# A decoder trunk on one Trainium2 core: a first pass with the scale's dot first, weights split behind the last heads, and modulation dots at other places

## The chip, the cores and the metric

The kernel runs on one core of a Trainium2 chip. The metric is device time in microseconds (us) for one execution, taken as the median of several runs; lower is better. A core has five engines that run their own instruction streams in order: TensorE (PE; its weight loads are listed as PEld), VectorE (DVE), ScalarE (ACT), GpSimd (POOL), and SyncE (SP), which here only issues DMAs. They meet at semaphores. An instruction that waits holds everything behind it on its engine.

## The reference

Two decoder layers on 256 tokens of width 1024, float32. Layer 0 mixes tokens by three dilated sliding-window attentions (16 heads of 64), layer 1 by gated linear attention (GLA, 4 heads, chunks of 64). A gated ConvFFN (inner width 2816) follows each. Every sub-layer is normed and modulated by a conditioning vector c:

```python
mod = silu(c) @ w_ada[i] + b_ada[i]
sh1, sc1, g1, sh2, sc2, g2 = split(mod, 6)
h = rmsnorm(x, norm_mix[i]) * (1 + sc1) + sh1
x = x + g1 * mixer(h)                  # attention, or GLA
h = rmsnorm(x, norm_ffn[i]) * (1 + sc2) + sh2
x = x + g2 * conv_ffn(h)
```

The modulation weights w_ada are 2 x 1024 x 6144 floats: 48 MB that are read once and used for a single vector.

## The kernel before, in words

Tokens lie along the free axis, features on the partitions, in KT = 8 tiles of 128 x 256. Every big product is done in three float32r products (`mm3`, lines 178 to 183): ScalarE rounds an operand to its high part (a cast, line 172), VectorE subtracts to get the low part (line 175), and TensorE adds high x high, low x high and high x low. So each weight chunk costs a DMA into one of four `raw` buffers, two casts on ScalarE (`whi`) and two subtractions on VectorE (`wlo`), all in `split` (line 156); `whi` and `wlo` have six buffers each.

Modulation isn't done on TensorE. `ada_chunk` (line 129) loads 1 MB of w_ada and does two dots with silu(c) on VectorE (line 138; a second small instruction reads the sum), and ScalarE adds the bias and makes the 128 x 1 column that the norm uses (lines 146 and 148): of scale or of shift. There are 48 chunks. The first eight make scale and shift of the first norm, one pair for each of the eight input tiles; the other forty are put between other work by `next_ada`.

First pass (lines 360 to 402, and 535 to 545): from the squares of x comes rstd (line 190). Then, for each of the eight input tiles (a block here), a chunk of modulation, `normed` (line 259: xr, high part hhi, low part hlo of the normed tile), and 15 x 128 columns of weights `w0`. A block feeds 42 products of TensorE, for the q, k of two head pairs and the v of one.

Then come eight head pairs (`attend`), the output projection with residual and squares (`project`, line 579), and the FFN (`ffn`, line 613), whose first two weight chunks are split early; the second waits in order behind the sixth tile's scaling (line 615). The norm's mean square is a product of TensorE over summed squares (`sqacc`, then `ms`, line 193).

In layer 1, four chunks of v weights are split and loaded (line 775; `next_ada` behind the third and fourth), then the decay gates, then for each head `states` (line 799): k_d, q_t, k_t from q, k and the gates (lines 818 to 820), k_d turned by TensorE (kdt, line 826), and the running states. `products` and `normed_output` (lines 859 and 873) make a head's output and its norm (osq, oacc, ms, on); `gate` (line 897) makes two tiles of the silu gate from 48 products (pr). Heads' outputs times gates give ohi and olo (lines 942 to 945) for `project`, whose products are py.

The order on each engine is fixed when the program is built: the Tile framework places instructions by its own estimate of time, and `behind(...)` only says that an instruction stands later in its engine's order than another one. It adds no wait.

Of the kernel before, what the change touches and what calls it, by code (L numbers as in the profile page):

```python
# [49 lines left out]

ADA_ORDER = [x for kt in range(KT) for x in ((0, kt), (1, kt))]
ADA_ORDER += [(2, kt) for kt in range(KT)]
# [5 lines left out]
def trunk(ctx: ExitStack, tc: tile.TileContext, I, out):  # L58
# [69 lines left out]

    def ada_chunk(l, n, dmas=1):
        raw = wraw.tile([P, 2048], F32, tag="raw", name="ada_raw")  # L130
        for i in range(dmas):
            c = slice(2048 * i // dmas, 2048 * (i + 1) // dmas)
            nc.sync.dma_start(raw[:, c], I["w_ada"][l, n][:, c])
        for s in range(2):
            piece, kt = ADA_ORDER[2 * n + s]
            dot = tmp.tile([P, 1], F32, tag="dot", name="dot", bufs=4)
            w = raw[:, D * s : D * s + D]
            nc.vector.tensor_tensor_reduce(  # L138
                w, w, c_bc, op0=ALU.mult, op1=ALU.add, scale=1.0, scalar=0.0, accum_out=dot,
            )  # L140
            m = state.tile([P, 1], F32, tag=f"mod{l}{piece}{kt}", name="mod")
            b = col(C_BADA + 48 * l + 8 * piece + kt)
            if piece in (1, 4):
                g = col((C_NMIX if piece == 1 else C_NFFN) + 8 * l + kt)
                b1 = (16 if piece == 4 else 0) + 8 * l + kt
                last = nc.scalar.activation(m, dot, AF.Identity, scale=g, bias=one_b[:, b1 : b1 + 1])
            else:
                last = nc.scalar.activation(m, dot, AF.Identity, bias=b)
            mod[l, piece, kt] = m
        return last  # L150

# [3 lines left out]

    def split(src, n, dmas=1, after=((), ()), late=(), low=(), cut=None):
        cut = cut or (n // 2 if n > 1024 else n)
        raw = wraw.tile([P, 2048], F32, tag="raw", name="raw")
        for c in (slice(0, cut), slice(cut, n)) if dmas > 1 else (slice(0, n),):
            last_load[0] = nc.sync.dma_start(raw[:, c], src[:, c])  # L160
        pieces = []
        for c in (slice(0, cut), slice(cut, n)):
            if c.stop > c.start:
                hi = wspl.tile([P, 1024], F32R, tag="whi", name="whi")
                lo = wspl.tile([P, 1024], F32R, tag="wlo", name="wlo")
                pieces.append((c.start, c.stop, hi, lo, raw[:, c]))
        ops = [(hi[:, 0 : b - a], lo[:, 0 : b - a], r) for a, b, hi, lo, r in pieces]
        if n == 1024:
            ops = [tuple(z[:, c] for z in ops[0]) for c in (slice(0, 512), slice(512, n))]
        for i, (hi, lo, r) in enumerate(ops):  # L170
            with behind(*after[i]):
                copied[0] = nc.scalar.copy(hi, r)  # L172
        for i, (hi, lo, r) in enumerate(ops):
            with behind(*(late if i else low)):
                last_lo[0] = nc.vector.tensor_tensor(lo, r, hi.bitcast(F32), op=ALU.subtract)  # L175
        return pieces

    def mm3(ps, a, b, start, stop):
# [79 lines left out]

    def normed(l, sub, r, kt):

        xr = tmp.tile([P, T], F32, tag="xr", name="xr")
        a, sh = mod[l, 3 * sub + 1, kt], mod[l, 3 * sub, kt]
        nc.vector.scalar_tensor_tensor(xr, x[kt], a[:, 0:1], r, op0=ALU.mult, op1=ALU.mult)
        hi, lo = h_hi[kt][:, :], h_lo[kt][:, :]
        i = nc.scalar.activation(hi, xr, AF.Identity, bias=sh[:, 0:1])  # L265
        j = nc.vector.scalar_tensor_tensor(
            lo, xr, sh[:, 0:1], hi.bitcast(F32), op0=ALU.add, op1=ALU.subtract
        )
        chain[kt] = chain[7] = i, j
        return h_hi[kt], h_lo[kt]  # L270
# [96 lines left out]
    for n in (0, 4):  # L367
        for m in (2, 1):
            s = sq[n // 4]
            last_add = nc.vector.tensor_tensor(s[:, 0:m, :], s[:, 0:m, :], s[:, m : 2 * m, :], op=ALU.add)  # L370
        if n == 0:
            with behind(last_add):
                last_add = scale_terms(0)
    exp_ln_after(last_sq)
    r = rstd_of([s[:, 0, :] for s in sq])

    rows_ps, at = [], 0
    with behind(norm_ops[0]):
        keep_warm(3)
        for i, (g, n) in enumerate(ROWS):  # L380
            c = slice(at, at + n)
            ps = bank("rows", "t")[:16, 0:n]
            rows_ps.append((ps, c))
            mm(ps, tab[:, 16 * g : 16 * g + 16], oh[:33, c], start=True, stop=True)
            at += n
    first = norm_ops[1], last_add
    w0, h = [], []
    for kt in range(KT):
        with behind(*first):
            term = ada_chunk(0, kt, dmas=1 if kt else 2)  # L390
        h.append(normed(0, 0, r, kt))
        if kt:
            w0.append(split(I["w0"][kt], 15 * P, cut=8 * P))
        else:
            with behind(chain[0][1]):
                w0.append(split(I["w0"][kt], 15 * P, 2, cut=8 * P, after=((term,), (chain[0][0],))))
# [3 lines left out]
            first = (last_lo[0],)  # L400
        if kt == 1:
            scale_terms(1)
    with tc.issue_after(last_load[0].ins):
# [11 lines left out]

    last_t, last_po = [None], [None]

    def attend(u, q, k, v, bias):
# [61 lines left out]
        src, hv, lv = in_order(po[:, :T]), as_tokens(hi), as_tokens(lo)  # L480
        nc.scalar.copy(hv, src)
        nc.vector.tensor_tensor(lv, src, hv.bitcast(F32), op=ALU.subtract)
        o_hi.append(hi)
# [35 lines left out]
    for u in range(NPAIR):  # L519
# [10 lines left out]
        if u == 0:  # L530
# [5 lines left out]
            for kt in range(KT):  # L536
                s, e = kt == 0, kt == KT - 1
                for i in range(2 * NG):
                    mm3(pqk[i][:, :T], parts(w0[kt], P * i), h[kt], s and i % 2 == 0, e and i % 2 == 1)
# [4 lines left out]
                for i in range(2 * NG):  # L544
                    mm3(pqk1[i], parts(w0[kt], P * (i + (6 if i < 2 else 9))), h[kt], s and i % 2 == 0, e and i % 2 == 1)
        if u < 2:
# [252 lines left out]
    def states(hd):  # L799
# [24 lines left out]
        for t in range(2):  # L824
            c = slice(P * t, P * t + P)
            nc.tensor.transpose(ps[:, c], k_d[:, c], ident)
        turned_keys[:] = nc.scalar.copy(kd, ps[:, :T]), last_key

        pa = bank("a", "s")
# [42 lines left out]

    def normed_output(hd, po, after=()):
# [3 lines left out]
        nc.vector.tensor_tensor(acc, sq[:, 0:T], sq[:, T : 2 * T], op=ALU.add)  # L877
        with behind(*after):
            rr = rstd_of([acc], 256, "s")
        on = gt([P, 2, T], f"on{hd}")  # L880
# [4 lines left out]

    r_g = []

# [9 lines left out]
    def gate(n):  # L897
        level = level_tiles() if n == 2 else ()

        w = split(I["w_r_b"][n], 2048, **({} if n else dict(after=(turned_keys[:1], ()), low=turned_keys[1:])))  # L900
        pr = bank("pr", "p")
        for kt in range(KT):
            for s in range(2):
                with behind(*((), last_o, norm_ops[:1], ())[n]):
                    mm3(pr[:, T * s : T * s + T], parts(w, 2 * P * kt + P * s),
                        level[kt] if n == 2 and kt < 2 else h[kt], kt == 0 and s == 0, kt == KT - 1 and s == 1)
        r = gt([P, (2, 3)[n % 2] * T], f"r{n}", tag=("r0", "C1", "r2", "cs1")[n])
        r_g.append(r[:, : 2 * T].rearrange("p (a b) -> p a b", a=2))
# [14 lines left out]
    gate(0)  # L923
    for _ in range(3):
        next_ada()
    po3 = products(3, *s3)
    normed_output(2, po2, last_o)
    normed_output(3, po3)
    gate(1)
    next_ada()  # L930
    for n in range(4):

        if n > 1:
            gate(n)
        r = r_g[n]
        if n < 2:
# [161 lines left out]
```

## Time and profile before

| | us |
|---|---|
| median of 3 runs | 791.72 (791.23 to 794.37) |
| the profiled execution | 792.91 |
| its span, first to last instruction | 791.1 |
| outside the span | 1.8 |
| TensorE busy | 772.1 |
| VectorE busy | 647.5 |
| ScalarE busy | 486.9 |

Times in rows are us from the span's start. A row of the timeline reads: start, duration, engine, line, operation, output and inputs by their names in the code, shapes, count (xN: so many in a row, the duration being from the first's start to the last's end), and in brackets the idle time of the engine just before it and what ended it. Pipelined instructions overlap their successors a little, so a step costs the distance of two starts rather than the printed duration. A row of a table of stretches reads: the stretch, its length, for each engine busy us and count, the granted TensorE clock as a share of full speed, the DMA engines' busy share, and GB/s.

### The profile page before, as it was taken

Reading aid. Unit: us, or ns where it says so; the run is one execution under the profiler, and the core shown is the slowest. Engines: PE = TensorE matmul, PEld = TensorE weight load, DVE = VectorE, ACT = ScalarE, POOL = GpSimd, SP = SyncE. Lnnn points to the kernel's source line nnn. Section 1 sums busy time; section 2 is a strip of 40 time slices with the busy share of each in tenths; the row PEclk is TensorE's granted clock in tenths of the full one; section 3 lists DMA queues with packets and bytes.
Section 4 is the critical chain, followed back from the end, with each engine's and each line's share of the span. In section 5 each row is a group of like instructions: output and inputs, shape, how many; then the busy total and the mean of one; then the engine's idle time right before and its main releaser. Section 6 shows DMA issues by size and latency. Waiting matters only on the chain.

```text
span 791.1 us, 15977 instructions
## 1 busy us (share of the span) xinstructions
PE 772.1 (98%) x6416; PEld 744.7 (94%) x6416; DVE 647.5 (82%) x1159; ACT 486.9 (62%) x939; POOL 12.2 (2%) x40
## 2 busy tenths in 40 slices
PE   8799999999999998999999999989999999999997
PEld 5799999999999997999999999888999999999997
DVE  6988988778788958999998776895777998899672
ACT  5546555555545647877666565654776876666551
POOL 1000000000000000000000000000000000000000
PEclk9899999999999999999999999999999999999999
DMA  9998576685775835767645895982544765555741
GB/s 350 418 331 331 157 312 218 232 317 196 270 273 197 302 141 172 285 239 264 218 146 197 301 323 188 329 303 86 214 165 156 258 206 184 206 195 183 274 150 54
DMA packets 32616, 184.72 MB, mean 233 GB/s; under 512 B 5852, under 2 KB 7388, under 8 KB 16286
## 3 DMA queue, kind: packets, MB, share of 16 engines
q1 hardware_dynamic: 32160, 183.26, 65.0%
q8 instruction: 50, 0.82, 0.4%
q10 hardware_dynamic: 382, 0.45, 0.2%
q14 instruction: 24, 0.20, 0.1%
HBM read 182.59 MB, written 1.10 MB: 232 GB/s over the span
## 4 chain that ended last, share of the span: by engine, by line
PE 90%; DVE 4%; ACT 3%; DMA 2%; issue 1%; ACTq 0%; DVEq 0%
PE pab L181 10%; PE pab L183 10%; PE pab L182 10%; PE pqk L181 7%; PE pqk L182 6%; PE pqk L183 6%; PE pd L183 5%; PE pd L182 5%; PE pd L181 5%; PE pv L181 3%; PE pv L183 2%; PE pv L182 2%; PE s L429 2%; PE py L181 2%; PE py L182 2%; PE py L183 2%
## 5 line engine op out<-in xcount | busy, mean ns | idle before, releaser
L172 ACT CAST whi<-raw 128x1024 fp32r<-128x1024 f32 (+3 forms) x273 | 252.5, 949 | 158.3 <-PE pab L182 56.0
L175 DVE TENSOR_TENSOR wlo<-raw,whi 128x1024 fp32r<-128x1024 f32 (+3 forms) x273 | 295.4, 1099 | 62.1 <-ACT whi L172 60.3
L183 PE MATMUL pab<-hhi,wlo 128*128 128x256 f32 x672 | 185.0, 276 | 0.0
L182 PE MATMUL pab<-hlo,whi 128*128 128x256 f32 x672 | 184.9, 276 | 0.0
L181 PE MATMUL pab<-hhi,whi 128*128 128x256 f32 x672 | 183.7, 277 | 0.0
L181 PE MATMUL pqk<-hhi,whi 128*128 128x256 f32 x440 | 122.6, 287 | 5.8 <-ACT hhi L265 5.8
L183 PEld LDWEIGHTS pab<-hhi,wlo 128*128 128x128 f32 x672 | 126.2, 188 | 0.0
L182 PEld LDWEIGHTS pab<-hlo,whi 128*128 128x128 f32 x672 | 126.1, 188 | 0.1
L181 PEld LDWEIGHTS pab<-hhi,whi 128*128 128x128 f32 x672 | 125.3, 188 | 0.1
L182 PE MATMUL pqk<-hlo,whi 128*128 128x256 f32 x440 | 123.6, 284 | 0.0
L183 PE MATMUL pqk<-hhi,wlo 128*128 128x256 f32 x440 | 123.0, 283 | 0.0
L138 DVE CUSTOM_DVE_ANT_0 ada_raw<-ada_raw,c_bc 128x1024 f32<-128x1024 f32 x96 | 113.5, 1219 | 9.6 <-DMA ada_raw<-in_w_ada 9.6
L183 PE MATMUL pd<-ghi,wlo 128*128 128x256 f32 x352 | 97.2, 276 | 0.0
L181 PE MATMUL pd<-ghi,whi 128*128 128x256 f32 x352 | 97.2, 276 | 0.0
L182 PE MATMUL pd<-glo,whi 128*128 128x256 f32 x352 | 97.2, 276 | 0.0
L181 PEld LDWEIGHTS pqk<-hhi,whi 128*128 128x128 f32 x440 | 83.1, 192 | 7.1 <-ACT hhi L265 6.2
L182 PEld LDWEIGHTS pqk<-hlo,whi 128*128 128x128 f32 x440 | 83.7, 191 | 0.8 <-issue 0.3
L183 PEld LDWEIGHTS pqk<-hhi,wlo 128*128 128x128 f32 x440 | 83.6, 191 | 0.5 <-issue 0.3
L181 PEld LDWEIGHTS pd<-ghi,whi 128*128 128x128 f32 x352 | 66.1, 188 | 0.0
L183 PEld LDWEIGHTS pd<-ghi,wlo 128*128 128x128 f32 x352 | 66.1, 188 | 0.0
L182 PEld LDWEIGHTS pd<-glo,whi 128*128 128x128 f32 x352 | 66.1, 188 | 0.0
L182 PE MATMUL pv<-wlo,hhi 128*128 128x384 f32 (+1 forms) x144 | 50.3, 349 | 0.0
(215 smaller groups left out, 1308.2 us busy)
## 6 DMA issues: line engine op xcount, KB each, us to landing
ada_raw<-in_w_ada SPq DMA_DIRECT2D x47, 1024.0 KB, 6.7
raw<-in_w_up SPq DMA_DIRECT2D x42, 1024.0 KB, 4.8
raw<-in_w_down SPq DMA_DIRECT2D x32, 704.0 KB, 5.0
raw<-in_wqk SPq DMA_DIRECT2D x18, 1024.0 KB, 6.7
raw<-in_wv SPq DMA_DIRECT2D x14, 768.0 KB, 4.8
raw<-in_w SPq DMA_DIRECT2D x7, 960.0 KB, 6.9
raw<-in_w_out_a SPq DMA_DIRECT2D x4, 1024.0 KB, 7.3
raw<-in_w_v_b SPq DMA_DIRECT2D x4, 1024.0 KB, 6.9
```

The lines of the kernel that those rows point to most:

```text
L138: nc.vector.tensor_tensor_reduce(w, w, c_bc, op0=ALU.mult, op1=ALU.add, scale=1.0, scalar=0.0, accum_out=dot,)
L172: copied[0] = nc.scalar.copy(hi, r)
L175: last_lo[0] = nc.vector.tensor_tensor(lo, r, hi.bitcast(F32), op=ALU.subtract)
L181: mm(ps, a[0], b[0], start=start, stop=False)
L182: mm(ps, a[0], b[1], start=False, stop=False)
L183: return mm(ps, a[1], b[0], start=False, stop=stop)
L429: mm(s[:, 0:n], q[0][a][:, r].rearrange("p a b -> p (a b)"), k[0][b][:, 0:n], start=(i == 0), stop=(i == 2))
```

## The change

It has these parts:

1. The order of modulation pieces is scale, shift instead of shift, scale. `ada_chunk` is divided into a load and single dots.
2. In the first pass a block's work is ordered by hand: scale's dot, the previous block's second low part, shift's dot, xr, first low part, hlo. In block 0 TensorE does the products with high parts of the normed tile first.
3. The second half of the squares goes to TensorE in four pieces instead of two additions on VectorE; six warm-up products are added ahead of the first pass.
4. The split of the FFN's second weight chunk in layer 0 is put behind the last head pair's output instead of behind the sixth tile's scaling, and its second low part no longer behind the residuals.
5. In layer 1 the six modulation chunks of the v weights and gates are placed behind k_t of heads 0, 1 and 2, behind head 3's sum of squares, and behind the low parts of gates 2 and 3. The norms of heads 2 and 3 come behind both gate(0) and gate(1).

```diff
-ADA_ORDER = [x for kt in range(KT) for x in ((0, kt), (1, kt))]
+ADA_ORDER = [x for kt in range(KT) for x in ((1, kt), (0, kt))]
...
-    r = rstd_of([s[:, 0, :] for s in sq])
+    r = rstd_of([sq[0][:, 0, :]] + [sq[1][:, i, :] for i in range(4)])
...
+    with behind(last_row):
+        keep_warm(6)
     w0, h = [], []
+    ada = ada_load(0, 0, 2)
+    with behind(norm_ops[1], last_add):
+        dots = [ada_dot(0, 0, s, ada) for s in range(2)]
     for kt in range(KT):
-        with behind(*first):
-            term = ada_chunk(0, kt, dmas=1 if kt else 2)
-        h.append(normed(0, 0, r, kt))
-        if kt:
-            w0.append(split(I["w0"][kt], 15 * P, cut=8 * P))
...
+        term = dots[1][1]
+        def between(scaled, high):
+            w0.append(split(I["w0"][kt], 15 * P, 1 if kt else 2, cut=8 * P, after=((term,), (high,)), lows=False))
+            with behind(scaled):
+                return [low_part(w0[-1], 0)]
+        h.append(normed(0, 0, r, kt, (dots[1][0],), between))
+        last = chain[kt][1]
...
+        if kt < KT - 1:
+            ada = ada_load(0, kt + 1)
+            with behind(last):
+                dots = [ada_dot(0, kt + 1, 0, ada)]
+            last = dots[0][0]
+        with behind(last):
+            last = low_part(w0[kt], 1)
...
+        if kt < KT - 1:
+            with behind(last):
+                dots.append(ada_dot(0, kt + 1, 1, ada))
...
-        with behind(*sixth):
-            w_early.append(split(I["w_up"][l, 1], 2048, late=last_x[1:]))
+        with behind(*(sixth if l else o_parts)):
+            w_early.append(split(I["w_up"][l, 1], 2048, late=last_x[1:] if l else ()))
...
             w = split(I["w_v_b"][n], 2048) if n else w_first
-            if n > 1:
-                next_ada()
...
         turned_keys[:] = nc.scalar.copy(kd, ps[:, :T]), last_key
+        if hd < 3:
+            with behind(last_key):
+                next_ada()
...
     gate(0)
-    for _ in range(3):
+    po3 = products(3, *s3)
+    gate(1)
+
+    normed_output(2, po2, within[3:4])
+    normed_output(3, po3, within[6:7], "t")
+    with behind(last_acc[0]):
         next_ada()
-    po3 = products(3, *s3)
-    normed_output(2, po2, last_o)
-    normed_output(3, po3)
-    gate(1)
-    next_ada()
     for n in range(4):
         if n > 1:
             gate(n)
+            with behind(last_lo[0]):
+                next_ada()
```

`ada_load` is the DMA of the old `ada_chunk`, `ada_dot` one dot with its term, `low_part` one subtraction of `split`. `within[k]` is the last product of a gate's k-th input tile.

The order of the changed program as built, where the diff doesn't say it. VectorE, a block of the first pass:

```
dot of scale (next block)   |  second low part (this block)  |  dot of shift (next block)
xr (next)  |  first low part (next)  |  hlo (next)  |  dot of scale (the one after) ...
```

ScalarE, the same stretch: scale's term, shift's term, first cast, hhi, second cast, and again. TensorE at the end of layer 1's heads: all 48 products of gate(1), the mean-square product of head 2, that of head 3, then gates 2 and 3, then py. VectorE there: oacc of head 3, four dots, two low parts, on of head 2 (two), two dots, on of head 3 (two), on x r of heads 0 and 1 (four) and of head 2 (one), a low part, on x r of head 2, two low parts, olo of tile 0. SyncE behind the first pass: first half of wv, eight bias loads with x among them, second half of wv, two chunks of modulation, wqk, a chunk of modulation, wqk, a chunk, four bias loads, wqk; before, both halves of wv stood ahead of the bias loads, and that last wqk too.

More of the change, by code (lines that the diff above doesn't have):

```diff
@@ L133, in ada_chunk, with ada_dot, split @@
             nc.sync.dma_start(raw[:, c], I["w_ada"][l, n][:, c])
-        for s in range(2):
[L135 to L150, printed above, removed]
+        return raw
+    def ada_dot(l, n, s, raw):
+        piece, kt = ADA_ORDER[2 * n + s]
+        dot = tmp.tile([P, 1], F32, tag="dot", name="dot", bufs=4)
+        w = raw[:, D * s : D * s + D]
+        i = nc.vector.tensor_tensor_reduce(
+            w, w, c_bc, op0=ALU.mult, op1=ALU.add, scale=1.0, scalar=0.0, accum_out=dot,
+        )
+        m = state.tile([P, 1], F32, tag=f"mod{l}{piece}{kt}", name="mod")
+        b = col(C_BADA + 48 * l + 8 * piece + kt)
+        if piece in (1, 4):
+            g = col((C_NMIX if piece == 1 else C_NFFN) + 8 * l + kt)
+            b1 = (16 if piece == 4 else 0) + 8 * l + kt
+            j = nc.scalar.activation(m, dot, AF.Identity, scale=g, bias=one_b[:, b1 : b1 + 1])
+        else:
+            j = nc.scalar.activation(m, dot, AF.Identity, bias=b)
+        mod[l, piece, kt] = m
+        return i, j
+    def ada_chunk(l, n):
+        raw = ada_load(l, n)
+        for s in range(2):
+            ada_dot(l, n, s, raw)
     last_load, copied, last_lo = [None], [None], [None]
-    def split(src, n, dmas=1, after=((), ()), late=(), low=(), cut=None):
+    def split(src, n, dmas=1, after=((), ()), late=(), low=(), cut=None, lows=True):
         cut = cut or (n // 2 if n > 1024 else n)
@@ L366, in trunk @@
             last_sq = nc.scalar.activation(sq[1][:, i - 4 : i - 2, :], x_all[:, i : i + 2, :], AF.Square)
[L367 to L373, printed above, removed]
+    for m in (2, 1):
+        last_add = nc.vector.tensor_tensor(sq[0][:, 0:m, :], sq[0][:, 0:m, :], sq[0][:, m : 2 * m, :], op=ALU.add)
+    with behind(last_add):
+        last_add = scale_terms(0)
     exp_ln_after(last_sq)
-    r = rstd_of([s[:, 0, :] for s in sq])
+    r = rstd_of([sq[0][:, 0, :]] + [sq[1][:, i, :] for i in range(4)])
     rows_ps, at = [], 0
@@ L383, in trunk @@
             rows_ps.append((ps, c))
-            mm(ps, tab[:, 16 * g : 16 * g + 16], oh[:33, c], start=True, stop=True)
+            last_row = mm(ps, tab[:, 16 * g : 16 * g + 16], oh[:33, c], start=True, stop=True)
             at += n
-    first = norm_ops[1], last_add
+    with behind(last_row):
+        keep_warm(6)
     w0, h = [], []
+    ada = ada_load(0, 0, 2)
+    with behind(norm_ops[1], last_add):
+        dots = [ada_dot(0, 0, s, ada) for s in range(2)]
     for kt in range(KT):
-        with behind(*first):
-            term = ada_chunk(0, kt, dmas=1 if kt else 2)
-        h.append(normed(0, 0, r, kt))
-        if kt:
-            w0.append(split(I["w0"][kt], 15 * P, cut=8 * P))
-        else:
-            with behind(chain[0][1]):
-                w0.append(split(I["w0"][kt], 15 * P, 2, cut=8 * P, after=((term,), (chain[0][0],))))
+        term = dots[1][1]
[5 more added lines that the diff above has]
+        last = chain[kt][1]
+        if kt == 0:
             with behind(copied[0]):
@@ L399, in trunk @@
                     nc.scalar.copy(rows[:, c], ps)
-            first = (last_lo[0],)
-        if kt == 1:
-            scale_terms(1)
+        if kt < KT - 1:
[5 more added lines that the diff above has]
+            last = low_part(w0[kt], 1)
+        if kt == 1:
+            with behind(last):
+                last = scale_terms(1)
+        if kt < KT - 1:
+            with behind(last):
+                dots.append(ada_dot(0, kt + 1, 1, ada))
     with tc.issue_after(last_load[0].ins):
@@ L537, in trunk @@
                 s, e = kt == 0, kt == KT - 1
-                for i in range(2 * NG):
-                    mm3(pqk[i][:, :T], parts(w0[kt], P * i), h[kt], s and i % 2 == 0, e and i % 2 == 1)
+                first = [(i, b, P * i) for i, b in enumerate(pqk)] + [(i, pqk1[i], P * (6 + i)) for i in range(2)]
+                if kt:
+                    for i, b, at in first:
+                        mm3(b, parts(w0[kt], at), h[kt], False, e and i % 2 == 1)
+                else:
+                    for low in range(2):
+                        for i, b, at in first:
+                            hi, lo = parts(w0[kt], at)
+                            if low:
+                                mm(b, hi, h[kt][1], start=False, stop=False)
+                            else:
+                                mm(b, hi, h[kt][0], start=i % 2 == 0, stop=False)
+                                mm(b, lo, h[kt][0], start=False, stop=False)
                 wv = parts(w0[kt], 8 * P, NG * P)
@@ L543, in trunk @@
                     mm3(pv[t][:, : NG * P], ht, wv, s, e)
-                for i in range(2 * NG):
-                    mm3(pqk1[i], parts(w0[kt], P * (i + (6 if i < 2 else 9))), h[kt], s and i % 2 == 0, e and i % 2 == 1)
+                for i in range(2, 2 * NG):
+                    mm3(pqk1[i], parts(w0[kt], P * (i + 9)), h[kt], s and i % 2 == 0, e and i % 2 == 1)
         if u < 2:
@@ L871, in products, with normed_output @@
         return po
-    def normed_output(hd, po, after=()):
+    def normed_output(hd, po, after=(), tag="s"):
         sq = gt([P, 2 * T], "osq", bufs=1)
@@ L884, in normed_output @@
         o_n.append(on)
-    r_g = []
+    r_g, within, last_acc = [], [], [None]
     def level_tiles():
```

33 lines of the change are left out of this document (20 added, 13 removed).

## The prediction

> **What bounds the kernel now.** I read the page's first part and the waits of TensorE first, then the granted clock around each wait. In a wait's row stand the engine and tile that waited, what released it, the sum in us, how often, and the longest.
>
> ```profile
> span 791.1 us, 15977 instructions
> PE 772.1 (98%) x6416; PEld 744.7 (94%) x6416; DVE 647.5 (82%) x1159; ACT 486.9 (62%) x939; POOL 12.2 (2%) x40
> ...
> PE pqk L181 <- ACT hhi L265: 5.8, 2, 5.4
> PE kdt L826 <- DVE k_d L818: 2.5, 1, 2.5
> PE ms L193 <- DVE sqacc L208: 2.3, 1, 2.3
> ...
> PE kv L842 <- ACT kdT L827: 0.7, 1, 0.7
> ```
>
> TensorE is busy for 98% of the span, so only its gaps can be won, and a new gap is paid in full. There are three long gaps. After each the clock is low: PEclk is the share of full speed granted in the stretch.
>
> ```profile
> 18.70:24.10 5.40, 0.00 (x0) 0.00 (x0) 5.40 (x9) 2.93 (x7) 0.00 (x0) 0.73 1.01 417
> 24.10:30.00 5.90, 5.88 (x32) 5.88 (x33) 5.90 (x10) 3.11 (x6) 0.00 (x0) 0.67 1.02 419
> ...
> 300.00:305.00 5.00, 4.79 (x13) 3.61 (x14) 3.50 (x8) 3.02 (x7) 0.00 (x0) 0.66 0.52 161
> ...
> 526.00:531.00 5.00, 5.00 (x27) 4.39 (x27) 5.00 (x9) 2.50 (x8) 0.00 (x0) 0.66 0.97 359
> ...
> 548.00:552.00 4.00, 3.28 (x24) 2.60 (x23) 2.08 (x4) 2.83 (x5) 0.31 (x1) 1.00 0.00 0
> ```
>
> A mean of 0.66 over 5 us is 3.4 us at half clock, in which 1.7 us of work are lost. So the gaps of 2.3 and 2.5 us cost about 4 us each, and the one of 0.7 us costs only itself. The change goes at all three long gaps.
>
> **The change part by part.** *First pass, steady state.* Before, one block (one eighth of the input width) takes VectorE this long:
>
> ```profile
> 35.89 0.48 DVE L263 SCALAR_TENSOR_TENSOR xr<-x_all,mod,rstd 128x256 f32<-128x256 f32 x1
> 36.29 1.22 DVE L138 CUSTOM_DVE_ANT_0 ada_raw<-ada_raw,c_bc 128x1024 f32<-128x1024 f32 x1
> 37.43 0.08 DVE L138 DVE_READ_ACCUMULATOR2_ANT dot<- 128x1 f32 x1
> 37.43 1.22 DVE L138 CUSTOM_DVE_ANT_0 ada_raw<-ada_raw,c_bc 128x1024 f32<-128x1024 f32 x1
> ...
> 38.58 0.48 DVE L266 SCALAR_TENSOR_TENSOR hlo<-xr,mod,hhi 128x256 fp32r<-128x256 f32 x1
> 38.98 2.22 DVE L175 TENSOR_TENSOR wlo<-raw,whi 128x1024 fp32r<-128x1024 f32 x2
> 41.11 0.48 DVE L263 SCALAR_TENSOR_TENSOR xr<-x_all,mod,rstd 128x256 f32<-128x256 f32 x1
> ```
>
> From xr to xr are 5.22 us without a pause; start to start, a dot takes 1.14 us, xr and hlo 0.40 each, and the two low parts together 2.13, which by columns is 1.14 and 1.00. TensorE needs 5.10 us for a block (the last one before, 44 products with the edges):
>
> ```profile
> 57.50:62.60 5.10, 5.10 (x44) 5.10 (x43) 3.80 (x7) 3.35 (x9) 0.00 (x0) 1.00 0.99 410
> ```
>
> The changed order closes a loop between the two engines. In the order as built, ScalarE does for each block: scale's term, shift's term, cast of the first weights, hhi, cast of the second. The cast thus stands behind the shift's dot, and VectorE's first low part waits for that cast. Behind the low part stand hlo, the next scale's dot, the second low part and the next shift's dot: nothing on VectorE can pass. The links:
>
> ```profile
> 32.66 1.90 ACT L172 CAST whi<-raw 128x1024 fp32r<-128x1024 f32 x2 [0.28 <-DMA raw<-in_w]
> ...
> 37.55 0.29 ACT L148 ACTIVATE mod<-dot,small 128x1 f32<-128x1 f32 x1 [0.63 <-DVE dot L138]
> 37.75 1.88 ACT L172 CAST whi<-raw 128x1024 fp32r<-128x1024 f32 x2
> ```
>
> ```profile
> 33.75 2.23 DVE L175 TENSOR_TENSOR wlo<-raw,whi 128x1024 fp32r<-128x1024 f32 x2 [0.16 <-ACT whi L172]
> ```
>
> Shift's dot to its term 0.12 (37.43 to 37.55), term to cast 0.20, cast to low part 1.09 (32.66 to 33.75), then 1.14 + 0.40 + 1.14 + 1.00 + 1.15: **6.24 us a block** instead of 5.22, and above TensorE's 5.10.
>
> *Where the loop starts.* The second half of the squares is no longer added on VectorE; the mean square takes five products in place of two, ten passes in place of four.
>
> ```profile
> 7.78 1.06 PE L193 MATMUL ms<-sq,ones_d 128*128 128x256 f32 x2
> ...
> 9.91 1.33 PE L276 MATMUL warm<-ones_d 128*128 128x128 f32 x6
> ```
>
> A row by line gives the shortest, median and longest of such a pass in ns, over the whole kernel:
>
> ```profile
> L193 PE MATMUL ms<-sq,ones_d x10: 379/634/795, 7.8 to 602.9; 128*128 128x256 f32 x10
> ```
>
> ```profile
> 10.15 0.47 ACT L195 ACTIVATE ln<-ms,eps 128x256 f32<-128x256 f32 x1 [1.20 <-PE ms L193]
> ...
> 11.46 1.03 ACT L172 CAST whi<-raw 128x1024 fp32r<-128x1024 f32 x1
> 12.39 0.50 ACT L265 ACTIVATE hhi<-xr,mod 128x256 fp32r<-128x256 f32 x1
> ```
>
> Two passes take 1.06 us and one 0.634, so they follow each other by 0.43 us at half clock. Ten from 7.78 end at 7.78 + 9 x 0.43 + 0.63 = 12.3, 2.1 later than ln's 10.15; at full clock, where a pass takes 0.38 and they follow by 0.21, at 7.78 + 9 x 0.21 + 0.38 = 10.1. Between 0 and +2.1 I take +1.6, nearer the end whose row is at half clock. The additions that VectorE saves buy nothing, since xr waits for rstd. Then, as before, cast at 11.46 + 1.6 = 13.1, first low part 14.2, hlo 15.3, dot 15.7, second low part 16.8, dot 17.8, its end 19.0. A block's first product comes 0.12 + 0.20 + 0.93 + 0.56 = 1.81 behind its shift's dot (cast to hhi 0.93; hhi at 12.39 to a product at 12.95): block 1 at 20.8 instead of 24.1, so the gap of 5.4 us does go. But block 7 comes at 19.0 + 6 x 6.24 + 0.1 (scale_terms) + 1.8 = 58.3. It takes 5.1, and 0.4 of waiting for its second cast, to 63.8, where before ended at 62.6: **+1.2**. The six more warm products (12 passes; by the row at 9.91, 1.33 us for six, about 2.6, at full clock half of it) lie under the loop: block 0 is done by about 21. Without that cover they would cost 1.3 to 2.6.
>
> *Behind the first pass.* The last low part ends near 60.5 (56.5 + 0.12 + 0.20 + 1.09 + 1.14 + 0.40 + 1.00) instead of 51.6 (41.1 + 2 x 5.22), so raw buffers come free 9 us later, and SyncE's order as built puts bias loads ahead of one half of wv and of the third pair's last wqk. Loads are late already:
>
> ```profile
> ACT whi L172 <- DMA raw<-in_wv: 29.5, 12, 4.4
> ...
> ACT whi L172 <- DMA raw<-in_wqk: 17.4, 10, 2.6
> ```
>
> TensorE now never waits for them. Bounds: 0, and one wait of wqk's longest, 2.6; I take **+1.4**, the middle, since 9 us is more than any of these waits.
>
> *Up-projection's weights behind the last heads.*
>
> ```profile
> 297.84 1.23 DVE L175 TENSOR_TENSOR wlo<-raw,whi 128x1024 fp32r<-128x1024 f32 x1 [0.45 <-ACT whi L172]
> 299.50 0.42 DVE L208 TENSOR_TENSOR sqacc<-sqacc,sq 128x256 f32<-128x256 f32 x1 [0.44 <-ACT sq L205]
> ```
>
> The low part leaves the path to sqacc, but a square on ScalarE is late next, and the casts there now stand ahead of the squares, waiting for buffers. Bounds 0 and the whole gap, -2.3, with 1.7 of clock; I take **-0.4**, because the row of the square's wait stays.
>
> By the Trainium skill ("TensorE: Matmul & The Clock Gate", Part 1) the clock falls to half only after a whole idle window of about 3.4 us. The trace disagrees: 2.3 us sufficed here. By that rule the remaining gap near 300 would leave the clock alone; this is a rival below.
>
> *Modulation behind k_t and gates.*
>
> ```profile
> 519.88 1.22 DVE L138 CUSTOM_DVE_ANT_0 ada_raw<-ada_raw,c_bc 128x1024 f32<-128x1024 f32 x1
> ...
> 522.17 1.75 DVE L760 TENSOR_TENSOR_SCAN cs<-keep,sp 128x768 f32<-128x768 f32 x1
> 523.84 1.20 DVE L175 TENSOR_TENSOR wlo<-raw,whi 128x1024 fp32r<-128x1024 f32 x1
> 524.95 0.42 DVE L818 TENSOR_TENSOR k_d<-pqk,e_d 128x256 f32<-128x256 f32 x1
> ```
>
> Two dots, 2.29 us, leave the way to k_d, which then starts at 522.7; two more chunks leave the stretch before it. The gap of 2.5 us and its 1.7 us of clock go: **-4.2**. The gap of 0.7 at kv stays.
>
> Their new place has a price. As built, both mean-square products of heads 2 and 3 stand behind the whole of gate(1). Head 3's sum (oacc, one buffer) waits for head 2's product, and four dots stand behind that sum. VectorE then does in order: oacc 0.35, 4 dots, 2 low parts, 2 of on2, 2 dots, 2 of on3, 4 times on x r, one more, low part, one more, 2 low parts, olo0. That is 0.35 + 6 x 1.145 + 5 x 1.14 + 4 x 0.40 + 6 x 0.35 + 0.35 = 17.0 us. TensorE from the same instant: 0.5 of waiting, 0.4 of product, then gates 2 and 3, 96 products at 0.113: 11.9 us, then the output projection, whose first low product needs olo0. Before, VectorE had olo0 at 572.87 and TensorE came at 579.58:
>
> ```profile
> 564.64 0.42 DVE L877 TENSOR_TENSOR oacc<-osq 128x256 f32<-128x256 f32 x1 [2.08 <-PE ms L193]
> ...
> 572.87 0.76 DVE L945 TENSOR_TENSOR olo<-on,ohi 128x256 fp32r<-128x256 f32 x2
> ```
>
> ```profile
> 579.58 0.28 PE L181 MATMUL py<-ohi,whi 128*128 128x256 f32 x1
> ```
>
> Now 17.0 - 11.9 less 0.5 of products done in between: a gap of 4.6, one stretch of half clock 1.7, and the 0.5 of waiting for head 3's sum: **+6.8**. The moved loads land in idle time (DMA share 0.00 at 548 to 552).
>
> **Sum**: 1.2 + 1.4 - 0.4 - 4.2 + 6.8 = **+4.8 us**. The profiled execution (792.91, of which 791.1 span) becomes 797.7. The median of the runs shown, 791.72, lies 1.2 below the profiled one, so I predict **796.5**.
>
> **Rivals.** *The tail is hidden* (not slower): if head 3's sum comes 5.1 us or more ahead of gate 2, VectorE's 17.0 us fit, and 6.8 fall away: 789.7. For it: VectorE is busy for only 2.08 of the 4 us from 548 to 552. Against: one buffer and the built order; 0.09. *The loop doesn't close*: if casts run ahead of the shift's dot, blocks take 5.22 from 20.8, the pass ends at 57.4 and nothing is late behind it: 796.5 - 6.4 - 1.4 = 788.7. Against it stands ScalarE's order; 0.05. *The clock stays up near 300*, the gap being too short for it: 794.8; for it the shorter gap, against it 2.3 us; 0.10. *The change doesn't do what it says*: later loads keep k_d late, and the 4.2 stay: 800.7; against it two chunks fewer before; 0.06. The forecast has 0.70.
>
> **How the numbers follow.** The forecast's own range is 793.0 to 800.3. Low: the mean square at its lower end (-1.6) and the w_up gap gone whole (-1.9). High: the mean square +0.5, later loads +1.2, w_up +0.4, a second half-clock window +1.7. It holds nearly all of the forecast and of the clock rival, 8 in 10. About 0.5% (4 us) is what a measurement of this kernel can tell from no change. Above 795.7 lie 0.59 of the forecast's 0.70, 0.03 of the clock rival and k_d's 0.06: slower 0.68. Same: 0.11 + 0.07 + 0.09 = 0.27. Faster 0.05.
>
> **What would show it.** In the changed profile: block starts 6.2 us apart with VectorE idle for 1 us ahead of each first low part, TensorE in block 1 near 21; no wait at kdt; a wait of over 4 us in two or three pieces at py, with a low clock behind it; a wait near 2 us at ms. Blocks 5.2 apart, or no wait at py, would make the prediction wrong.

## The result, and the profile after

The changed kernel takes 804.52 us (median of 6 executions, 802.73 to 806.20), and the kernel before, executed beside it, 793.13 (791.23 to 794.73). The ratio is 1.0145 with a 95% interval of 1.0122 to 1.0168: slower by 11.4 us, where +4.8 was predicted. The predicted range ended at 800.3. The profiled execution of the changed kernel is the shortest of the six, with 802.73 us and a span of 800.9, so its trace has to explain +9.8 against the span of 791.1 before; the remaining 1.6 are in executions without a trace.

The page of the changed kernel and its waits of TensorE (engine, tile and line that waited, what released it, sum in us, how often, longest):

```profile
span 800.9 us, 16016 instructions
PE 780.4 (97%) x6434; PEld 748.7 (93%) x6434; DVE 645.5 (81%) x1157; ACT 486.9 (61%) x939; POOL 13.1 (2%) x40
```

```profile
PE py L194 <- DVE olo L991: 2.9, 1, 2.9
PE pqk L193 <- ACT hhi L278: 2.5, 7, 0.5
...
PE ms L205 <- DVE sqacc L220: 1.7, 1, 1.7
PE pv L193 <- ACT whi L179: 1.1, 1, 1.1
PE py L193 <- ACT r L958: 1.0, 1, 1.0
...
PE pqk L193 <- ACT v L543: 0.6, 1, 0.6
PE ms L205 <- DVE oacc L919: 0.6, 1, 0.6
PE pv L194 <- DVE wlo L182: 0.5, 1, 0.5
PE pv L193 <- ACT v L543: 0.4, 1, 0.4
```

The waits of 5.4 us in the first pass and of 2.5 at kdt are gone. New are seven of at most 0.5 in the first pass, three at pv (the second pair's value products, just behind the pass), one at the next pair's pqk, one at ms and two at py. The granted clock (the column behind the engines' busy times; stretch, length, busy times, clock, DMA share, GB/s) shows half clock in three stretches; a mean of 0.83 over 10 us is 1.7 us lost:

```profile
66.00:76.00 10.00, 8.35 (x39) 7.78 (x39) 7.49 (x13) 4.00 (x10) 0.00 (x0) 0.83 1.01 423
302.00:312.00 10.00, 8.08 (x36) 6.36 (x35) 7.00 (x17) 7.19 (x19) 1.98 (x2) 0.83 0.30 107
...
580.00:595.00 15.00, 11.09 (x79) 10.49 (x78) 12.13 (x26) 8.82 (x18) 0.00 (x0) 0.89 0.59 221
```

The first of these is where the prediction had no lost clock at all. To put a size to each term, I took the start of the same product in both traces and followed how far the changed kernel is behind:

| Stretch, up to the first product of | before | changed | behind | term measured | predicted |
|---|---|---|---|---|---|
| the value products of pair 1 (first pass ends) | 62.70 | 64.49 | +1.79 | +1.8 | +1.2 |
| the output projection behind the last head pair | 287.94 | 294.53 | +6.59 | **+4.8** | **+1.4** |
| the first up-projection | 305.52 | 311.87 | +6.35 | -0.2 | -0.4 |
| head 3's states in the GLA layer (end of the wait at kv) | 550.08 | 552.88 | +2.80 | -3.6 | -4.2 |
| the last up-projection | 605.54 | 615.38 | +9.84 | +7.0 | +6.8 |

Four of the five terms are right to 0.7 us. The second is wrong by 3.4.

### The profile page after: what moved, and what is told of

Read it like the earlier page. It is cut to its first block, busy times and chain, and to the rows that moved or that the text cites. A ratio compares the mean times of both kernels' runs of the same rounds, so it can differ in the third digit from the quotient of the medians.

```text
span 800.9 us, 16016 instructions
## 1 busy us (share of the span) xinstructions
PE 780.4 (97%) x6434; PEld 748.7 (93%) x6434; DVE 645.5 (81%) x1157; ACT 486.9 (61%) x939; POOL 13.1 (2%) x40
## 4 chain that ended last, share of the span: by engine, by line
PE 68%; DVE 14%; DMA 9%; ACT 5%; issue 3%; SPq 1%; ACTq 0%; DVEq 0%
PE pab L194 10%; PE pab L195 10%; PE pab L193 10%; PE pd L194 5%; PE pd L195 5%; PE pd L193 5%; DMA raw<-in_wqk 4%; DVE wlo L182 4%; DMA raw<-in_wv 4%; DVE ada_raw L140 3%; ACT whi L179 2%; PE py L194 2%; PE py L193 2%; PE py L195 2%; PE pv L195 2%
## 5 line engine op out<-in xcount | busy, mean ns | idle before, releaser
L182 DVE TENSOR_TENSOR wlo<-raw,whi 128x1024 fp32r<-128x1024 f32 (+2 forms) x257 | 277.0, 1094 | 62.0 <-ACT whi L179 60.0
L193 PE MATMUL pqk<-hhi,whi 128*128 128x256 f32 x432 | 118.1, 284 | 3.2 <-ACT hhi L278 2.5
L194 PE MATMUL pqk<-hlo,whi 128*128 128x256 f32 x432 | 119.2, 282 | 0.0
L195 PE MATMUL pqk<-hhi,wlo 128*128 128x256 f32 x432 | 119.0, 281 | 0.0
L193 PEld LDWEIGHTS pqk<-hhi,whi 128*128 128x128 f32 x432 | 79.7, 188 | 5.4 <-ACT hhi L278 4.0
L194 PEld LDWEIGHTS pqk<-hlo,whi 128*128 128x128 f32 x432 | 80.7, 188 | 1.1 <-issue 0.7
L195 PEld LDWEIGHTS pqk<-hhi,wlo 128*128 128x128 f32 x432 | 80.7, 188 | 0.5 <-issue 0.3
L193 PE MATMUL pv<-whi,hhi 128*128 128x384 f32 (+1 forms) x144 | 50.3, 357 | 1.5 <-ACT whi L179 1.1
```

Source lines behind the costliest of these rows:

```text
L193: mm(ps, a[0], b[0], start=start, stop=False)
L194: mm(ps, a[0], b[1], start=False, stop=False)
L195: return mm(ps, a[1], b[0], start=False, stop=stop)
```

## The experiments

Eleven kernels ran, in three sets (four, four and three, in the order below), each set beside its own executions of the kernel before (medians 793.23, 792.89 and 792.49). Where two kernels of different sets are compared, a difference of their medians can be off by the 0.7 us between these. The line numbers in their rows are their own.

**wv_first** (wv's loads ahead of the bias loads). The rows of SyncE's queue in the changed kernel say why I tried it (start, us, queue, line, transfer):

```profile
50.57 0.38 SPq L167 DMA_DIRECT2D raw<-in_wv  x1
54.20 0.52 SPq L368 DMA_DIRECT2D bias<-rows_d  x1
...
58.07 0.54 SPq L434 DMA_DIRECT2D x_all<-in_xT  x1
...
59.84 0.54 SPq L167 DMA_DIRECT2D raw<-in_wv  x1
```

The second half of pair 1's weights leaves at 59.84, behind eight bias loads and x_all. The same load left before 46.8 in the kernel before.

```diff
+    ahead = [load_raw(I["wv"][0, half], 1536, 768) for half in range(2)]
     for u in range(NPAIR):
         with tc.issue_after(last_load[0].ins):
             bias = load_bias(u)
...
-                    w = split(I["wv"][u - 1, half], 1536)
+                    w = split(I["wv"][u - 1, half], 1536, raw=ahead[half] if u == 1 else None)
```

> The changed kernel with both of wv's first two loads issued on SyncE ahead of the bias loads of the first two pairs; nothing else differs. Theory A (queue order): in the changed kernel the second wv load left SyncE at 59.84 though its buffer was free at about 55.4 (end of block 6's second low part), because eight bias loads from 54.20 on and x_all stood ahead of it; the 1.65 us of waits at pv and the half clock behind them (1.7 us) are its price. Expected: 804.5 - 3.3 = 801.2, second wv load issued before 56.5, no wait over 0.6 at pv, full clock from 66 to 76. Theory B (late buffers): the load is late because the pass frees its buffers late, whatever stands in the queue; waits at pv and clock stay, 804.5.

Measured: 803.86 (799.74 to 806.85, 4 executions), ratio 1.0130 (1.0089 to 1.0171). In the profile both wv loads leave ahead of the bias loads, the second by 56.3, and the wait at pv for weights is gone: theory A has the cause of *that wait* right. The time doesn't confirm its price. The profiled execution (806.85, the longest) comes out of the value products 3.5 us earlier than the changed kernel, but reaches the output projection behind the last head pair at 296.31, 1.8 later. In between it loses 3.4 us to a low clock behind waits of 0.4 us, and another wait of 1.0 at 250. Waits from 60 to 90, and the clock:

```profile
PE s L464 <- DVE k L538: 0.4, 1, 0.4
PE pqk L198 <- ACT whi L184: 0.4, 1, 0.4
PE s L464 <- DVE m L482: 0.4, 1, 0.4
PE pv L198 <- ACT v L548: 0.2, 1, 0.2
```

```profile
76.00:84.00 8.00, 7.21 (x43) 6.29 (x42) 6.10 (x17) 4.65 (x12) 0.20 (x2) 0.57 0.92 358
```

**cast_first** (the loop of the first pass broken).

```diff
-            w0.append(split(..., after=((term,), (high,)), lows=False))
+            w0.append(split(..., after=((dots[0][1],), (high,)), lows=False))
```

> The changed kernel with the first cast of each block placed behind the scale's term instead of the shift's; nothing else differs. Theory A (the loop sets the pace): blocks 5.2 apart instead of 6.2, VectorE without a pause ahead of the first low part, the pass ends near 58 instead of 64.1; 804.5 - 6.1 = 798.4 with the wait at wv's weights as it is, and down to 793.8 if that wait (4.6 us between the pass and the output projection) goes with it. Rival C (the loads set the pace: DMA share 0.89, 333 GB/s in the pass): blocks stay 6.2 apart, 804.5.

Measured: 798.16 (796.85 to 799.91), ratio 1.0062 (1.0042 to 1.0082), 6.4 us faster than the changed kernel, the number of theory A. But it isn't reached in the way that A said, so the number is luck. hhi of successive blocks comes 5.3 to 6.8 us apart, 6.0 in the mean, in place of 6.2; the cast now waits for its load, which is rival C:

```profile
42.31 1.05 ACT L179 CAST whi<-raw 128x1024 fp32r<-128x1024 f32 x1 [1.25 <-DMA raw<-in_w]
...
55.82 1.05 ACT L179 CAST whi<-raw 128x1024 fp32r<-128x1024 f32 x1 [2.89 <-DMA raw<-in_w]
```

The pass ends at 63.45 in the profile (with a first load that came 0.6 later than in the changed kernel's), but TensorE waits 1.2 there for copies, and the value products start at 64.65, no earlier than in the changed kernel (64.49). So in the profile all of the gain lies behind the pass: no wait at pv for weights, and full clock from 62 to 72. The loop was real, but with it gone the loads hold the pace nearly as much.

**gla_before** (GLA stage as before, the rest changed).

> The changed kernel with the modulation and the mean squares of heads 2 and 3 in the GLA stage placed as before; the first pass and the split of w_up stay changed. Theory A: the tail's 7.4 us go and the 4.0 us at kdt come back: 804.5 - 7.4 + 4.0 = 801.1, a wait of about 2.5 at kdt, none at py. Rival D (the tail waits because weights or loads arrive late after the longer first pass, not because of the order behind head 3's sum): the wait at py stays and kdt's comes back, 808.5.

Measured: 798.86 (796.17 to 800.55), ratio 1.0071 (1.0046 to 1.0097). kdt's wait is back and py has none, so rival D is dead: the tail's wait belongs to the tail's own order. It is 2.2 faster than theory A said, within what the two intervals leave open. Its profile shows the wait at pv again, and longer than in the changed kernel:

```profile
PE pv L193 <- ACT whi L179: 3.9, 1, 3.9
...
PE kdt L867 <- DVE k_d L859: 2.3, 1, 2.3
```

SyncE's queue in gla_before says why it is longer. The write of rows_d leaves at 49.70, as in the changed kernel (49.58), but the first bias load, which reads it, leaves at 56.25 and not at 54.20, and so the weights behind the bias loads leave 3.0 later. The queue's own waits have 5.2 us for rows_d here and 3.2 in the changed kernel, which is 2.0 of it; the other 1.0 is one bias load that took 1.55 of the queue instead of 0.60:

```profile
49.70 0.42 SPq L435 DMA_DIRECT2D rows_d<-rows  x1
...
56.25 0.52 SPq L368 DMA_DIRECT2D bias<-rows_d  x1
...
62.85 0.54 SPq L167 DMA_DIRECT2D raw<-in_wv  x1
```

**only_late** (first pass as before; up-projection's split and GLA stage changed).

> The first pass as before (order of the dots, low parts, squares and products in block 0), with only the changed split of w_up and the changed GLA stage. Theory A (the parts add up): 793.1 - 0.25 - 4.0 + 7.4 = 796.3, the same waits at py as in the changed kernel. Rival D (tail late because of the first pass): no wait at py, 793.1 - 4.25 = 788.9.

Measured: 796.87 (796.26 to 798.31, 8 executions), ratio 1.0047 (1.0033 to 1.0061): theory A to 0.6 us. py waits 3.9 us, in three pieces, without any change in the first pass; in the changed kernel it was 3.9 in two:

```profile
PE py L187 <- DVE olo L954: 2.1, 1, 2.1
...
PE py L186 <- ACT r L921: 0.9, 1, 0.9
PE py L186 <- ACT ohi L953: 0.9, 1, 0.9
...
PE ms L198 <- DVE oacc L882: 0.6, 1, 0.6
```

**late_no_tail** takes the tail's part away from only_late.

```diff
     gate(0)
+    for _ in range(3):
+        next_ada()
     po3 = products(3, *s3)
+    normed_output(2, po2, last_o)
+    normed_output(3, po3)
     gate(1)
-    normed_output(2, po2, within[3:4])
-    normed_output(3, po3, within[6:7], "t")
-    with behind(last_acc[0]):
-        next_ada()
     for n in range(4):
         if n > 1:
             gate(n)
-            with behind(last_lo[0]):
-                next_ada()
```

> First pass as before; w_up's split and the modulation behind k_t of heads 0 to 2 as changed; the mean squares of heads 2 and 3 as before, and the three other chunks of modulation behind gate(0) as before (none behind head 3's sum or gates 2 and 3). Theory A: kdt's gap and its half clock go (-4.2), w_up -0.3, no new wait at py: 793.2 - 4.5 = 788.7. Rival E (the chunks behind k_t only move the wait, to the next head's products or to py): within 1 us of 793.2, with a wait of 1 us or more at o, kv or py that before has not.

Measured: 790.94 (788.72 to 793.24, 12 executions), ratio 0.9977 (0.9965 to 0.9990). The tail's placement is thus worth 796.87 - 790.94 = 5.9 us (5.6 when each is first taken against the kernel before of its own set). The gain at kdt is smaller than A said, and rival E is half right: a new wait of 1.2 stands at ms near 548.5, since eight dots run on VectorE between 536.7 and 547.3, ahead of the sum that this product reads:

```profile
PE ms L198 <- DVE oacc L882: 1.2, 1, 1.2
```

**late_chunks_out** has the mean squares of heads 2 and 3 placed as in the changed kernel, and only the six dots out of the tail (late_no_tail without its second pair of added lines and the first pair of removed ones).

> As late_no_tail, but with the mean squares of heads 2 and 3 placed inside gate(1) as in the changed kernel; only the six dots behind head 3's sum and behind gates 2 and 3 are out of the tail. Theory A (VectorE's queue of 17.0 us, of which the dots are 6.9, is the price): the gap at py goes, 0.6 of waiting at ms for head 3's sum stays: 788.7 + 0.6 = 789.3. Rival F (the later mean squares by themselves make olo0 late): a wait of over 2 us at py stays, 793 or more.

Measured: 791.72 (789.31 to 796.13), ratio 0.9994 (0.9981 to 1.0008). No wait at py, so F is out: the dots are nearly the whole price of the tail (5.2 of 5.9, or 4.8 of 5.6 set by set), and the later mean squares add a wait of 0.5 at ms for head 3's sum, as predicted for that piece.

**late_fill** puts products on ones, whose result nobody uses, into the wait at the up-projection's mean square.

```diff
         products(range(2))
+        keep_warm_t(8)
         r = rstd_of([sums[0], sums[1]], tag="p")
```

> The kernel of only_late (first pass as before, the rest changed) with 8 products on ones (16 passes, some 1.7 us) put into TensorE's wait at the mean square of the up-projection; their result is not used. Theory A (the half clock there follows from the idle time): no stretch of half clock between 295 and 310, 796.9 - 1.7 = 795.2. Rival G (the half clock there comes from something other than the wait): it stays, 796.9 to 797.3.

Measured: 799.24 (797.95 to 799.86). The function is called at three places, so two fillers of 16 passes (0.11 us each, 1.8 together) stand where there is nothing to fill; the expectation should have been 796.9 - 1.7 + 3.5 = 798.7. Near 300, where it was meant to be, the clock is full (below, for p4_fill, the same filler at the one place).

**combo**: cast_first and wv_first together, with late_no_tail's GLA stage.

> The changed first pass with its cast behind the scale's term and wv's loads ahead of the bias loads, and the GLA stage of late_no_tail. Theory A (parts add up): cast_first's 798.2 less what late_no_tail gains on only_late (8.2) less the 1.2 of waiting at pv: 788.8. Rival H (behind the first pass the loads stay late whatever their order): 790.0 or more, with waits between 60 and 130.

Measured: 792.73 (789.51 to 795.61, 10 executions), ratio 0.9993 (0.9976 to 1.0010). Rival H: just behind the pass TensorE waits once more, now for the copies of the first pair's values out of the accumulators. On ScalarE these stand behind two casts, and the casts waited for the second half of wv, so a late load is at the start of this wait too:

```profile
PE pv L198 <- ACT v L548: 2.5, 1, 2.5
```

```profile
59.88 1.57 ACT L184 CAST whi<-raw 128x768 fp32r<-128x768 f32 x2 [1.18 <-DMA raw<-in_wv]
```

**pass_wv_first** is gla_before with wv_first's edit.

> gla_before (GLA stage as before) with wv's first two loads issued ahead of the bias loads, so that the tail no longer scatters the time. Theory A (the second wv load stands behind bias loads): gla_before's profile has 4.4 us of waits at pv and one stretch of half clock behind them (1.7); both go and nothing else comes late: 798.9 - 6.1 = 792.8, and at least 3 below 798.9 if only the waits of the changed kernel's profile (1.65) and the clock go. Rival B2 (the stretch behind the pass is short of loads as a whole; the order only decides which product waits): no wait at pv, but others of 0.4 us and more between 70 and 80 and half clock behind them; within 1.5 of 798.9.

Measured: 796.69 (795.37 to 797.93, 6 executions), ratio 1.0055 (1.0041 to 1.0068): 2.2 below gla_before, or 1.4 when each is taken against its own set's kernel before. A said at least 3, B2 at most 1.5, and the intervals overlap. The waits at pv for weights are gone and the clock is full, which is A; waits of 0.3 and 0.7 stand at 76 to 78 in their place, which is B2. The queue's order is shown to make the wait at pv; its worth, 1.4 to 2.2 us, is not certain.

**p4** places the chunks where VectorE idles in the changed kernel's profile: one behind k_t of each of heads 0 to 2, two behind head 2's sum, one after gate(1); otherwise late_no_tail.

```diff
-    for _ in range(3):
-        next_ada()
     po3 = products(3, *s3)
     normed_output(2, po2, last_o)
+    acc2 = last_acc[0]
+    with behind(last_acc[0]):
+        for _ in range(2):
+            next_ada()
     normed_output(3, po3)
     gate(1)
+    for _ in range(1):
+        next_ada()
```

> First pass as before; w_up's split as changed; six chunks of modulation: one behind k_t of each of heads 0 to 2, two behind head 2's sum (where VectorE idles 2.1 and 3.5 us in the changed kernel's profile), one after gate(1); mean squares in the order of before. Theory A: kdt's wait and clock go, no 1.2 us wait at ms near 548 as in late_no_tail, and no wait at py: 792.9 - 3.5 - 0.3 = 789.1. Rival E (any chunk placed there makes something else late): a new wait of 1 us or more, 790.5 or more.

Measured: 789.50 (788.32 to 792.65, 12 executions), ratio 0.9961 (0.9950 to 0.9972): theory A to 0.4 us. The wait of 1.2 is gone, nothing stands at py, and one of 0.7 stands at ms for head 3's sum.

**p4_fill** is p4 with the filler at the first up-projection alone.

> p4 with 8 products on ones (16 passes) in TensorE's wait at the mean square of the first up-projection only. Theory A (half clock follows from idle time): p4 less 1.7 = 787.4, full clock from 295 to 310. Rival G: same as p4.

Measured: 788.05 (787.70 to 790.82, 6 executions), ratio 0.9952 (0.9937 to 0.9966): the fastest kernel here, 0.5% ahead of before and 2% ahead of the changed one. Over p4 it gains 1.45, with intervals that overlap. The wait is filled and the clock is full; both profiles with the filler have full clock there, but so have three of the eleven without (gla_before, late_chunks_out, pass_wv_first), so the filler's part is likely rather than shown. First p4, then p4_fill:

```profile
300.00:305.00 5.00, 4.80 (x15) 3.57 (x14) 2.75 (x8) 3.22 (x8) 0.00 (x0) 0.66 0.03 11
```

```profile
300.00:305.00 5.00, 4.84 (x28) 4.38 (x29) 3.15 (x8) 3.22 (x8) 0.00 (x0) 1.00 0.12 20
```

## Why the prediction was wrong, step by step

*The loop of the first pass: right.* 6.24 us a block were worked out, 6.22 measured. VectorE in one block of the changed kernel (idle time before an instruction and its releaser in brackets):

```profile
45.40 1.23 DVE L187 TENSOR_TENSOR wlo<-raw,whi 128x1024 fp32r<-128x1024 f32 x1 [0.90 <-ACT whi L179]
46.55 0.48 DVE L280 SCALAR_TENSOR_TENSOR hlo<-xr,mod,hhi 128x256 fp32r<-128x256 f32 x1
46.94 1.22 DVE L140 CUSTOM_DVE_ANT_0 ada_raw<-ada_raw,c_bc 128x1024 f32<-128x1024 f32 x1
...
48.09 1.09 DVE L187 TENSOR_TENSOR wlo<-raw,whi 128x896 fp32r<-128x896 f32 x1
49.09 1.22 DVE L140 CUSTOM_DVE_ANT_0 ada_raw<-ada_raw,c_bc 128x1024 f32<-128x1024 f32 x1
...
50.24 0.48 DVE L276 SCALAR_TENSOR_TENSOR xr<-x_all,mod,rstd 128x256 f32<-128x256 f32 x1
51.62 1.22 DVE L187 TENSOR_TENSOR wlo<-raw,whi 128x1024 fp32r<-128x1024 f32 x1 [0.91 <-ACT whi L179]
```

From 45.40 to 51.62, with 0.9 of idling ahead of the low part, as predicted. Block 1 starts on TensorE at 20.89 (20.8 predicted), block 7 at 58.26 (58.3). The start moved by 1.5, from xr at 11.6 to 13.1 (1.6). The pass's products end 1.2 later, and another 0.4 is a wait of the first value product for the copies out of the accumulators, which I had not counted. What the prediction had wrong here is the other case: it gave a kernel without the loop 5.22 us a block, and cast_first's blocks, without it, took 6.0, because its casts wait for their loads.

*Behind the first pass: the step that failed.* I had put +1.4, the middle (1.3, to be exact) between nothing and "one wait of wqk's longest, 2.6". The stretch cost 4.8. The idle time alone kept that bound: 1.10 and 0.55 at pv and 0.61 at the next pair, 2.3 in all.

```profile
67.06 1.56 ACT L179 CAST whi<-raw 128x768 fp32r<-128x768 f32 x2 [1.81 <-DMA raw<-in_wv]
```

```profile
67.95 0.44 PE L193 MATMUL pv<-whi,hhi 128*128 128x384 f32 x1 [1.10 <-ACT whi L179]
68.94 0.45 PE L194 MATMUL pv<-wlo,hhi 128*128 128x384 f32 x1 [0.55 <-DVE wlo L182]
```

What I left out, and so put at nothing, is the half clock behind them, 1.7 us, though I had paid it for every other long wait. With it the term is 4.0. A wait also costs more than the idle time in its row: from the start of the product before these two waits (66.51) to the start of the one behind them (69.22) are 2.71 us, for three steps that take 0.17 each undisturbed, so 2.2 where the rows say 1.65. That makes 4.5; 0.3 of the 4.8 stay unexplained. I had also taken the loads to be 9 us later, as the buffers are. The second one was 13 later, since it leaves behind eight bias loads: I had named that order and given it no price. And the wait isn't always the same: 1.65 in the changed kernel's profile, 4.4 in gla_before's, with the same first pass, mostly by how long SyncE's queue waits for the write of rows_d ahead of the bias loads.

By the medians this stretch and the pass cost 5.6 together (gla_before over before, with the -0.2 of the up-projection in it), where 2.6 - 0.4 was predicted. wv_first, cast_first and combo each took one wait away, and something else came late: the softmax's reading of earlier scores, loads for the pass, the copies of the first pair. Which share each has isn't settled.

*Up-projection's weights: right.* The wait at ms fell from 2.3 to 1.7, the term is -0.2 for -0.4. The half clock stayed, against the rival that gave it up; that was partly luck, since gla_before, with the same program up to there, has a wait of 1.9 and full clock (below).

*kdt: right, a little large.* Wait and half clock went; -3.6 for -4.2. p4 shows the same 3.5 without the changed first pass and tail. Where the other 0.6 went isn't known.

*The tail: right.* VectorE from the idle stretches behind head 2's sum over head 3's sum to olo0, and the products that wait for it:

```profile
565.19 2.36 DVE L182 TENSOR_TENSOR wlo<-raw,whi 128x1024 fp32r<-128x1024 f32 x2 [2.10 <-ACT whi L179]
571.09 0.43 DVE L919 TENSOR_TENSOR oacc<-osq 128x256 f32<-128x256 f32 x1 [3.54 <-PE ms L205]
...
587.56 0.41 DVE L991 TENSOR_TENSOR olo<-on,ohi 128x256 fp32r<-128x256 f32 x1
```

```profile
583.26 0.50 PE L193 MATMUL py<-ohi,whi 128*128 128x256 f32 x2
584.75 0.38 PE L193 MATMUL py<-ohi,whi 128*128 128x256 f32 x1 [0.99 <-ACT r L958]
588.03 0.55 PE L194 MATMUL py<-olo,whi 128*128 128x256 f32 x1 [2.90 <-DVE olo L991]
```

From head 3's sum the chain takes 16.8 us (17.0 worked out), TensorE 12.2 from the same instant (11.9 worked out, with the 0.5 of waiting in it; the terms given add up to 11.8). The whole is nearer than its parts: the idle time is 3.9 at py and 0.6 at ms, where 4.6 and 0.5 were forecast, and with 1.7 of clock that is 6.2 of the 7.0. Here too a wait costs some 0.3 more than its row says (584.75 to 588.03 are 3.28 us for a step that takes 0.11 undisturbed, so 3.17 for 2.90), and three such waits make up the rest. The rival "the tail is hidden" failed on the place that the trace of before shows and that I had named: head 3's sum waits 3.5 us for head 2's product. What scatters is the clock behind it: one stretch of half clock in the changed kernel's profile, two in only_late's (mean 0.69 over the 11 us from 576, 3.4 lost), so 1.7 or 3.4 for the same 3.9 us of waits at py:

```profile
576.00:587.00 11.00, 7.70 (x38) 7.30 (x39) 8.29 (x16) 5.23 (x11) 0.00 (x0) 0.69 0.53 181
```

*From the profiled execution to the median.* I took one offset for both kernels. Before, the profiled execution is a typical one; of the changed kernel it is the shortest, by 1.8 against the median. A kernel with more waits has more places at which the clock may fall, and a wait at pv that differs between executions. This is a likely reason and not a shown one, since no other execution of it has a trace. It belonged into the range on its upper side: 800.3 held one more stretch of half clock, and it needed one behind the first pass, one in the tail and the longer wait at pv.

## What to carry to other kernels

Give every wait that you predict on TensorE its lost clock as well, as a step of its own (nothing, 1.7 or 3.4 us here) and not only the waits that the old trace already shows with a low clock. Work moved behind a late sum can cost TensorE most of its time: here the sum waited for a product, and six dots behind it, 6.9 us on VectorE, cost about 5. Look for the stretch in which the engine idles (2.1 and 3.5 us here, behind head 2's sum) and put it there, as p4 did. And in a stretch in which loads, casts and copies are all just in time, advancing one of them gained less than its wait here; wv_first, pass_wv_first and combo all stayed behind their sums, as the next in line took its place.

## What the runs showed of the hardware

Half clock comes in stretches of 3.41 us or twice that, and their starts lie whole multiples of 3.413 us apart: 69.27, 308.20 and 588.09 in the changed kernel's trace, 70 and 82 steps. The same wait of 1.9 us at ms brought half clock in p4 (0.66, above) and none in gla_before and late_chunks_out:

```profile
306.00:312.00 6.00, 3.89 (x18) 2.76 (x17) 3.00 (x8) 4.08 (x12) 0.53 (x1) 1.00 0.46 178
```

In those two a border of the 3.413 us grid, counted from their other stretches, falls into the wait and cuts it into parts of at most 1.1. In the thirteen traces, from 30 us on, 22 cells of the grid hold 1.5 us or more of TensorE's idle time, and behind 19 of them the next cell ran at half clock. The three others hold 1.83 (gla_before, at pv), 1.85 (combo, at pv) and 1.71 us (pass_wv_first, at ms). And in wv_first half clock came behind a cell with 0.8 us, in two waits of 0.4. So the idle time within a cell tells most of it, but isn't the whole rule, which stays open. The Trainium skill ("TensorE: Matmul & The Clock Gate", Part 1) has the cell, 3413 ns and free-running, and the trace agrees; it has the clock fall after a whole idle cell, and here less than half of one was enough.
